# Layer 0's residual held in units of 1/r while down products are added, GpSimd converting it both ways; layer 0's wide product groups ordered in runs of three

## The chip, the cores and the metric

One Trainium2 chip, of which the program uses one core. The metric is device time in microseconds (us) of one execution, lower is better. Beside the timed runs there is one profiled execution, and all durations below are from it.

## The reference, cut to what matters

A two-layer decoder trunk over 512 tokens, model width 1024, float32. Each layer has a mixer and then a gated convolutional FFN of width 2816; each adds its output to the residual `h`. The FFN is the part that the change touches:

```python
hn = rms_norm(h, norm_ffn[layer])          # h times r per token, times a gain per feature
g  = causal_dwconv3(hn @ w_gate, conv_w) + conv_b
h  = h + (silu(g) * (hn @ w_up)) @ w_down
```

The factor r of the norm is one number per token. It has to be inside the silu, so the gate takes it before the convolution. The up branch is linear in it, so r may be applied to the up product, to the gate's result, or to the whole output of the down product.

## The kernel before, in words

**Layout.** Features lie on the 128 partitions, tokens along the free axis. `h` is eight tiles of 128x512 (`h[0]` to `h[7]`), and the factor is a 128x512 tile `self.r` (`rstd_f` in the trace) with the same row on every partition, written by ScalarE (L222). Matrix products are float32 made of three products of a high and a low part: `hi` is a rounded copy by ScalarE, `lo` the rest, made either on VectorE (a subtraction, L152 or L857) or by a copy of minus the source on ScalarE and an adding DMA that GpSimd issues (`summed`, L141 to L145, and L887 to L889).

**The FFN of a layer.** `Ffn.steps` goes over the 22 column tiles of the FFN by two: f = 0, 2, 4, ... 20. f = 0 is computed directly (`direct`). From f = 2 on, gate and up are made by seven products of half size each (a block scheme), fourteen products a step, in `products` (L903 to L984), after `prepare` (L861) has loaded the weights, added and subtracted blocks on VectorE and split them. Between these steps stand groups of the down projection (`half_down`): two tiles after f = 2 and f = 4, four tiles after each later step, each for one half of the model width. Their results are added to `h` by VectorE (L314, `done` of `project`). The last four tiles of layer 0 go down in `d_last`, after f = 20, and there the next norm is begun.

**Wide products.** In most steps the two products with a high part as the stationary operand are made in one pass of 512 columns (high and low parts of the moving operand beside each other), and the product with the low part in one of 256 columns. `in_both` says where: in layer 0 wholly from f = 8, in layer 1 wholly from f = 6. Where a step is wholly wide, layer 1 orders the passes in runs of three (three of 256 columns, then three of 512, L949); layer 0 alternates pairs (L954).

**Who applies r.** In layer 1 the factor is given to the sum in the down step (`add`, L1371). In layer 0 VectorE multiplies: in `direct` each of the two gate results (L791); in `products` the second gate result (L971) and the first two up blocks (L973), beside the row that goes into the convolution, which both layers multiply (L968).

**What sets the order.** The program text gives a priority; a planner builds each engine's queue from it, taking at each free moment the first ready instruction by its own cost model. `behind(a, b)` asks that a stand after b in the queue, without a wait. On the chip every engine then takes its queue in order: GpSimd's holds the adding DMAs, so whatever stands in front of one delays it. `last_added[0]` is the last adding DMA of `summed`. Buffers: seven PSUM banks turn for all products, four `raw`, six `whi`, six `wlo`.

Of the kernel before, what the change touches and what calls it, by code (L numbers as in the profile page):

```python
# [8 lines left out]
F32 = mybir.dt.float32  # L9
# [3 lines left out]
ALU = mybir.AluOpType  # L13
PSUM = bass.MemoryType.PSUM

P = 128
D = 1024
S = 512
NK = D // P
NT = S // P  # L20
FF = 2816
NF = FF // P
# [9 lines left out]
def tile_trunk(ctx: ExitStack, tc: tile.TileContext, x, norm_mix, norm_ffn, final_norm,  # L32
# [3 lines left out]
    nc = tc.nc  # L36
# [9 lines left out]
    def mm_bank(name):  # L46
        return ps_mm.tile([P, 512], F32, tag="mm", name=name)
# [33 lines left out]
    def behind(ins, first):  # L81

        if first is not None:
            tc.add_manual_dep(ins.ins, first.ins.name, mybir.DependencyInfo(
                mybir.DependencyClass.NoSync, mybir.DependencyReason.DATA), reason="order")
# [49 lines left out]
    last_added = [None]  # L135
# [49 lines left out]
    h = [cp.tile([P, S], F32, tag=f"h{k}", name=f"h{k}") for k in range(NK)]  # L185
# [3 lines left out]
    def hg_k(k):  # L189
        return hg[k][0], hg[k][1]  # L190
# [525 lines left out]
    class Ffn:  # L716
# [52 lines left out]
        def direct(self, ch, before):  # L769

            layer = self.layer
            banks = {}
            for i, k in enumerate(PAIRS):
                for j in range(4):
                    before(i, j)
                    hi, lo = ch["gu"[j // 2], i // 4]
                    c = slice((j % 2) * P, (j % 2 + 1) * P)
                    if j not in banks:
                        banks[j] = mm_bank(f"gu{layer}_{j}")
                    mm3(banks[j], (hi[:, i % 4, c], lo[:, i % 4, c]), hg_k(k),  # L780
                        i == 0, i == NK - 1)

            def evacuate():
                r = self.r
                gates = []
                for j in range(2):
                    t = padded_tile()
                    nc.vector.tensor_tensor(t[:, 2:], banks[j], r, ALU.mult)
                    s = self.silu(self.conv(t, j), j)
                    if layer == 0:  # L790
                        nc.vector.tensor_tensor(s, s, r, ALU.mult)  # L791
                    gates.append(s)
                for j, s in enumerate(gates):
                    nc.vector.tensor_tensor(s, banks[2 + j], s, ALU.mult)
                return [(j, s) for j, s in enumerate(gates)]

            return evacuate
# [114 lines left out]
        def products(self, f, stat):  # L912

            layer, ap, n = self.layer, self.ap, f"{self.layer}_{f}"
            banks = {"g": {}, "u": {}}
            kept = ap.tile([P, 3, HALF], F32, tag="kept", bufs=1, name=f"kept{n}")
            pads = [padded_tile() for _ in range(2)]
            lo, hi = slice(2, 2 + HALF), slice(2 + HALF, 2 + S)
            dst = {("g", 1): pads[0][:, lo], ("g", 6): pads[0][:, hi], ("g", 7): pads[1][:, hi],
                   ("g", 4): pads[1][:, lo]}  # L920
            dst.update({("u", product): kept[:, i, :] for i, product in enumerate((1, 6, 7))})
            onto = {2: 1, 7: 7, 3: 6}
            s = {}

            def in_both(key, product):
                first = FIRST_WIDE[layer]
                return f >= first[key] or f == first["g"] and product in (2, 5, 3)

            def add(d, bank, halves):
                ins = None  # L930
                for half in halves:
                    ins = nc.vector.tensor_tensor(d, bank[:, half * HALF : (half + 1) * HALF], d,
                                                  ALU.add)
                return ins

            def after(key, product, bank):
                halves = range(1 + in_both(key, product))
                if product in onto:
                    ins = add(dst[key, onto[product]], bank, halves)
                    if product == 7:  # L940
                        self.added[key] = ins
                elif (key, product) != ("u", 4):
                    d = dst[key, 7 if product == 5 else product]
                    nc.scalar.copy(d, bank[:, :HALF])
                    add(d, bank, halves[1:])

            todo = [("g", 1), ("u", 1), ("g", 2), ("g", 5), ("g", 6), ("u", 5), ("u", 6),
                    ("g", 7), ("u", 2), ("u", 7), ("g", 3), ("u", 3), ("g", 4), ("u", 4)]
            if layer and all(in_both(*at) for at in todo):  # L949
                parts_of = [(0, (False,))]  # L950
                for i in range(0, len(todo), 3):
                    parts_of += [(j, (True,)) for j in range(i, min(i + 3, len(todo)))]
                    parts_of += [(j, (False,)) for j in range(i + 1, min(i + 4, len(todo)))]
            else:  # L954
                parts_of = [(i, (i % 2 == 1, i % 2 == 0)) for i in range(len(todo))]
            begun = set()
            for i, lows in parts_of:
                key, product = todo[i]
                bank = self.multiply(banks[key], f"{key}{n}", product, stat[key, product],
                                     in_both(key, product), lows)  # L960
                if len(lows) == 1 and i not in begun:
                    begun.add(i)
                    continue
                after(key, product, bank)
                if (key, product) in (("g", 4), ("g", 3)):
                    j = product == 4
                    row = pads[j][:, 2:]
                    nc.vector.tensor_tensor(row, row, self.r, ALU.mult)  # L968
                    s[j] = self.silu(self.conv(pads[j], f + j), f + j)
                    if j and layer == 0:  # L970
                        nc.vector.tensor_tensor(s[1], s[1], self.r, ALU.mult)  # L971
            if layer == 0:
                nc.vector.tensor_tensor(kept[:, :2, :], kept[:, :2, :],  # L973
                                        self.r.rearrange("p (a b) -> p a b", a=2), ALU.mult)
            s0 = s[0].rearrange("p (a b) -> p a b", a=2)
            nc.vector.tensor_tensor(s0, kept[:, :2, :], s0, ALU.mult)
            nc.vector.tensor_tensor(s[1][:, HALF:], kept[:, 2, :], s[1][:, HALF:], ALU.mult)
            last = bank[:, :HALF]
            if in_both("u", 4):
                last = kept[:, 0, :]  # L980
                nc.scalar.copy(last, bank[:, :HALF])
                add(last, bank, (1,))
            nc.vector.tensor_tensor(s[1][:, :HALF], last, s[1][:, :HALF], ALU.mult)
            return [(f + 1, s[1]), (f, s[0])]  # L984

        def hidden(self, f, before=lambda i, j: None):

            if f == 0:
                def first(i, j):
                    before(i, j)  # L990
                    if (i, j) == (3, 0):
                        nc.vector.tensor_copy(self.cols, self.norm.rstd_cols(inorder))
                    elif (i, j) == (6, 0):
                        self.r = self.norm.rstd_spread(inorder)

                ch = self.pair_weights([("g", 0), ("u", 0), ("g", 1), ("u", 1)])
                rest = self.direct(ch, first)
                for kp in range(NP):
                    self.block_sums(kp)
                self.second = self.prepare(2)  # L1000
                return rest()
            return self.products(f, self.second if f == 2 else self.prepare(f))

        def steps(self, half_down, before=lambda i, j: None):
# [11 lines left out]
        def split_acts(self, rows):  # L1016
            for ft, row in rows:
                self.act(ft, row)

    def ffn0(norm):  # L1020
        nonlocal prm1
        with tc.tile_pool(name="f0", bufs=1) as ap:
            def sums(kp):
                return [ap.tile([P, 2, HALF], F32R, name=f"t{i}_{kp}") for i in (2, 3)]

            ffn = Ffn(0, prm0, norm, ap, sums)
            def half_down(a, b, half):
                project(f"d0_{a}", w_ffn_down[0], ffn.acts, list(range(a, b)), None,
                        halves=(half,), tail=0)

            ffn.split_acts(ffn.steps(half_down))
            prm1 = params1(lambda ins: behind(ins, last_matmul[0]))
            nxt = Norm("m1", lambda k: prm1("mix", k))
            project("d0_last", w_ffn_down[0], ffn.acts, list(range(NF - 4, NF)), nxt)
            return nxt
# [588 lines left out]
```

## Time and profile before

| what | value |
|---|---|
| timed runs, median of 3 | 967.45 us (966.96 to 967.5) |
| the profiled execution's own time | 967.03 us |
| its span, first to last instruction | 965.2 us |
| TensorE (PE) busy | 956.3 us, 99% of the span |
| VectorE (DVE) busy | 847.2 us, 88% |
| ScalarE (ACT) busy | 619.9 us, 64% |
| GpSimd (POOL) busy | 162.3 us, 17% |
| granted TensorE clock | 0.997 |

How to read it: a row of the timeline has start, duration, engine, line of the kernel, operation, out<-in, shapes, and in brackets the idle time in front of it and who ended that. Where a row merges several instructions (x3), the duration is that of all. A row of a group has the count, then busy time and the mean in ns of one. A tile's name has no number of its step (`s12g` is that of every f), but PSUM banks have: `g_4b` is a bank of the gate at f = 4.

### The profile page before, as it was taken

Reading aid. Unit: us, or ns where it says so; the run is one execution under the profiler, and the core shown is the slowest. Engines: PE = TensorE matmul, PEld = TensorE weight load, DVE = VectorE, ACT = ScalarE, POOL = GpSimd, SP = SyncE. Lnnn points to the kernel's source line nnn. Section 1 sums busy time; section 2 is a strip of 40 time slices with the busy share of each in tenths; the row PEclk is TensorE's granted clock in tenths of the full one; section 3 lists DMA queues with packets and bytes.
Section 4 is the critical chain, followed back from the end, with each engine's and each line's share of the span. In section 5 each row is a group of like instructions: output and inputs, shape, how many; then the busy total and the mean of one; then the engine's idle time right before and its main releaser. Section 6 shows DMA issues by size and latency. Waiting matters only on the chain.

```text
span 965.2 us, 14237 instructions
## 1 busy us (share of the span) xinstructions
PE 956.3 (99%) x5155; PEld 826.9 (86%) x5155; DVE 847.2 (88%) x1435; ACT 619.9 (64%) x943; POOL 162.3 (17%) x184
## 2 busy tenths in 40 slices
PE   9999999999999999999999999999999999999996
PEld 7888898998888888888888888989888888888885
DVE  6887998989898998998878689889998989989897
ACT  5524667766575665765487847787665566646776
POOL 3141333111011010110311002321110011100123
PEclk9999999999999999999999999999999999999998
DMA  7442355787677677774452323567776777667865
GB/s 253 153 134 87 66 152 117 178 191 181 166 178 169 158 178 191 168 180 133 131 153 88 109 88 88 142 137 181 183 185 175 179 175 174 173 164 181 203 148 147
DMA packets 95537, 150.45 MB, mean 156 GB/s; under 512 B 5252, under 2 KB 61036, under 8 KB 95468
## 3 DMA queue, kind: packets, MB, share of 16 engines
q1 hardware_dynamic: 78140, 98.69, 32.9%
q0 software_dynamic: 15696, 49.03, 27.8%
q10 hardware_dynamic: 1632, 1.84, 0.6%
q8 instruction: 40, 0.66, 0.3%
q14 instruction: 29, 0.24, 0.1%
HBM read 98.42 MB, written 2.10 MB: 104 GB/s over the span
## 4 chain that ended last, share of the span: by engine, by line
PE 98%; DVE 1%; DMA 1%; issue 0%; ACT 0%; ACTq 0%
PE dn L156 3%; PE d L156 3%; PE d L157 3%; PE dn L157 3%; PE dn L158 3%; PE d L158 3%; PE vu_a L1166 2%; PE gu L156 2%; PE gu L158 2%; PE gu L157 2%; PE u_2a L705 1%; PE u_4a L705 1%; PE g_2a L705 1%; PE u_20a L695 1%; PE u_18a L695 1%; PE u_8a L695 1%
## 5 line engine op out<-in xcount | busy, mean ns | idle before, releaser
L143 POOL DMA_DIRECT2D wlo_g<-raw_g x20 | 17.2, 859 | 318.8 <-ACT wlo_g L141 95.0
L741 DVE SCALAR_TENSOR_TENSOR c<-rows,prm,c 128x512 f32<-128x512 f32 x88 | 65.2, 750 | 1.4 <-ACT c L739 1.2
L156 PE MATMUL d<-a_hi,whi_d 128*128 128x512 f32 x144 | 56.2, 390 | 0.0
L156 PE MATMUL dn<-whi_dn,a_hi 128*128 128x512 f32 x144 | 56.1, 390 | 0.0
L157 PE MATMUL d<-a_lo,whi_d 128*128 128x512 f32 x144 | 56.1, 390 | 0.0
L157 PE MATMUL dn<-wlo_dn,a_hi 128*128 128x512 f32 x144 | 56.1, 390 | 0.0
L158 PE MATMUL d<-a_hi,wlo_d 128*128 128x512 f32 x144 | 56.1, 389 | 0.0
L158 PE MATMUL dn<-whi_dn,a_lo 128*128 128x512 f32 x144 | 56.1, 389 | 0.0
L856 ACT ACTIVATE whi_a<-raw_g 128x512 fp32r<-128x512 f32 x20 | 12.6, 632 | 67.3 <-PE g_18e L695 9.4
L739 ACT ACTIVATE c<-rows,prm 128x512 f32<-128x512 f32 x44 | 31.3, 714 | 10.6 <-DVE rows L968 10.6
L1371 DVE SCALAR_TENSOR_TENSOR y<-dn,small,y 128x512 f32<-128x512 f32 x40 | 28.0, 749 | 6.6 <-PE dn L158 6.6
L749 ACT ACTIVATE s<-c,prm 128x512 f32<-128x512 f32 x44 | 31.4, 716 | 3.1 <-DVE c L741 3.0
L265 ACT ACTIVATE a_hi<-s 128x512 fp32r<-128x512 f32 x40 | 24.8, 626 | 12.0 <-PE d L158 9.4
L201 ACT ACTIVATE hg<-h,prm 128x512 fp32r<-128x512 f32 x24 | 17.3, 719 | 23.5 <-DVE h L314 17.0
L158 PEld LDWEIGHTS d<-a_hi,wlo_d 128*128 128x128 f32 x144 | 27.1, 188 | 5.6
L158 PEld LDWEIGHTS dn<-whi_dn,a_lo 128*128 128x128 f32 x144 | 27.0, 188 | 5.6
L156 PEld LDWEIGHTS d<-a_hi,whi_d 128*128 128x128 f32 x144 | 27.1, 188 | 5.6
L157 PEld LDWEIGHTS dn<-wlo_dn,a_hi 128*128 128x128 f32 x144 | 27.1, 188 | 5.6
L156 PEld LDWEIGHTS dn<-whi_dn,a_hi 128*128 128x128 f32 x144 | 27.1, 188 | 5.6
L157 PEld LDWEIGHTS d<-a_lo,whi_d 128*128 128x128 f32 x144 | 27.1, 188 | 5.5
L141 ACT ACTIVATE wlo_g<-raw_g 128x1024 fp32r<-128x1024 f32 x20 | 21.0, 1049 | 16.4 <-PE g_2e L705 7.7
L888 POOL DMA_DIRECT2D wlo_s34g<-s34g x18 | 15.5, 860 | 90.9 <-ACT wlo_s34g L887 64.6
(1280 smaller groups left out, 3387.7 us busy)
## 6 DMA issues: line engine op xcount, KB each, us to landing
raw_g<-in_w_ffn_gate_dram SPq DMA_DIRECT2D x40, 512.0 KB, 3.8
raw_u<-in_w_ffn_up_dram SPq DMA_DIRECT2D x40, 512.0 KB, 3.7
raw_dn<-in_w_ffn_down_dram SPq DMA_DIRECT2D x22, 512.0 KB, 3.6
wlo_g<-raw_g POOLq DMA_DIRECT2D x20, 512.0 KB, 5.2
wlo_u<-raw_u POOLq DMA_DIRECT2D x20, 512.0 KB, 6.1
raw_d<-in_w_ffn_down_dram SPq DMA_DIRECT2D x18, 512.0 KB, 4.1
wlo_s12g<-s12g POOLq DMA_DIRECT2D x18, 512.0 KB, 6.6
wlo_s34g<-s34g POOLq DMA_DIRECT2D x18, 512.0 KB, 5.6
```

What stands on the lines that cost most here:

```text
L141: first = nc.scalar.activation(lo, raw, AF.Copy, scale=-1.0)
L156: nc.tensor.matmul(ps, lhs[0], rhs[0], start=start, stop=False, skip_group_check=skip)
L157: nc.tensor.matmul(ps, lhs[0], rhs[1], start=False, stop=False, skip_group_check=skip)
L158: nc.tensor.matmul(ps, lhs[1], rhs[0], start=False, stop=stop, skip_group_check=skip)
L265: nc.scalar.activation(hi, src, AF.Copy, scale=scale)
L695: last_matmul[0] = nc.tensor.matmul(ps if low else banks[at], left(kp)[low], right(kp)[0] if low else both(kp), start=first, stop=kp == NP ...
L705: nc.tensor.matmul(ps, l, r, start=first, stop=end, skip_group_check=True)
L739: nc.scalar.activation(c, t[:, 0:S], AF.Copy, scale=prm("cf", ft))
L741: self.last_conv = nc.vector.scalar_tensor_tensor(c, t[:, i : S + i], prm("cf", i * NF + ft), c, op0=ALU.mult, op1=ALU.add)
L749: self.last_silu = nc.scalar.activation(s, c, AF.Silu, bias=self.prm("bf", ft))
L1166: nc.tensor.matmul(banks[at], lhs[l], rhs[r], start=first, stop=end, skip_group_check=True)
L1371: return nc.vector.scalar_tensor_tensor(dst, ps, ffn.cols[:, t : t + 1], dst, op0=ALU.mult, op1=ALU.add)
```

## The change

Before the first down group, layer 0's `h` is divided by r: VectorE makes `inverse` = 1/r (128x512) and GpSimd multiplies the eight `h` tiles by it, placed behind `prepare(2)`'s last adding DMA. While `h` is held so, down products are added without r, so the multiplications L791, L971 and L973 fall away for f = 0 to 16. For f = 18 and 20 they stay, since these tiles go down in `d_last`, by which time `h` has been multiplied by r again: four tiles on GpSimd after each half of the group that ends at tile 17. And layer 0's wholly wide steps (f = 8 to 20) take the order in runs of three.

```diff
                     s = self.silu(self.conv(t, j), j)
-                    if layer == 0:
-                        nc.vector.tensor_tensor(s, s, r, ALU.mult)
                     gates.append(s)
...
+            scale_up = layer == 0 and f >= NF - 4
...
-            if layer and all(in_both(*at) for at in todo):
+            if all(in_both(*at) for at in todo):
...
-                    if j and layer == 0:
+                    if j and scale_up:
                         nc.vector.tensor_tensor(s[1], s[1], self.r, ALU.mult)
-            if layer == 0:
+            if scale_up:
                 nc.vector.tensor_tensor(kept[:, :2, :], kept[:, :2, :],
                                         self.r.rearrange("p (a b) -> p a b", a=2), ALU.mult)
...
-                return rest()
+                rows = rest()
+                if self.layer == 0:
+                    self.unscale()
+                return rows
...
+        def unscale(self):
+            inverse = self.ap.tile([P, S], F32, name="inverse")
+            nc.vector.reciprocal(inverse, self.r)
+            for k in range(NK):
+                behind(nc.gpsimd.tensor_tensor(h[k], h[k], inverse, ALU.mult), last_added[0])
+
+        def rescale(self, half):
+            for k in range(4 * half, 4 * half + 4):
+                nc.gpsimd.tensor_tensor(h[k], h[k], self.r, ALU.mult)
...
                 project(f"d0_{a}", w_ffn_down[0], ffn.acts, list(range(a, b)), None,
                         halves=(half,), tail=0)
+                if b == NF - 4:
+                    ffn.rescale(half)
```

## The prediction

> **What bounds the kernel now.** I read the page first, its busy times and its chain.
>
> ```profile
> span 965.2 us, 14237 instructions
> ...
> PE 956.3 (99%) x5155; PEld 826.9 (86%) x5155; DVE 847.2 (88%) x1435; ACT 619.9 (64%) x943; POOL 162.3 (17%) x184
> ...
> PE 98%; DVE 1%; DMA 1%; issue 0%; ACT 0%; ACTq 0%
> ```
>
> TensorE stands on 98% of the chain that ended last. VectorE's 88% costs nothing until TensorE waits for it. So the change can gain only where it makes TensorE's own work shorter or takes away one of its few waits, and it can lose wherever it makes an operand late. What the new order is worth can be read in this profile, because layer 1 has it and layer 0 has not. The chain of waits in order of time shows the same place of successive steps:
>
> ```profile
> 279.25 1.41 PE u_10a L695 x8
> ...
> 310.19 1.41 PE u_12a L695 x8
> ...
> 340.63 1.41 PE u_14a L695 x8
> ...
> 804.63 1.41 PE u_12a L695 x8
> 835.03 1.41 PE u_14a L695 x8
> ```
>
> A wide step of layer 0 in pairs takes 340.63 - 310.19 = 30.44 us, one of layer 1 in runs of three 835.03 - 804.63 = 30.40 us. One step of layer 0 is longer, f = 10: 310.19 - 279.25 = 30.94 us, so 0.50 more. The timelines of TensorE and VectorE show why:
>
> ```profile
> 293.90 0.69 DVE L877 TENSOR_TENSOR s12g<-raw_g,raw_g 128x512 f32<-128x512 f32 x1 [2.88 <-DMA raw_g<-in_w_ffn_gate_dram]
> ...
> 296.24 0.74 PE L695 MATMUL u_10a<-t,wlo_u 128*128 128x256 f32 x4 [0.23 <-DVE kept L932]
> ```
>
> VectorE stood 2.88 us for a late load, the emptying of a PSUM bank stood behind it in the queue, and TensorE waited for the bank.
>
> Then I looked at how much room VectorE has, in windows one step long: f = 2 with its down group, f = 4 with its own, and f = 20 (columns: length, PE, PEld, DVE, ACT, POOL busy with counts, clock, DMA).
>
> ```profile
> 165.50:191.13 25.63, 25.63 (x195) 24.67 (x194) 25.43 (x42) 20.34 (x32) 3.44 (x4) 1.00 0.69 166
> 191.13:216.59 25.46, 25.46 (x193) 24.51 (x192) 22.58 (x38) 18.12 (x28) 3.44 (x4) 1.00 0.82 197
> ...
> 430.41:460.85 30.44, 30.44 (x162) 26.18 (x160) 26.93 (x47) 16.04 (x24) 0.02 (x1) 1.00 0.54 148
> ```
>
> In the window of f = 2, VectorE is busy 25.43 of 25.63 us. That is the very place where the division by r is put.
>
> **What goes.**
>
> ```profile
> L971 DVE TENSOR_TENSOR s<-s,rstd_f 128x512 f32<-128x512 f32 x10 | 6.9, 692 | 0.0
> L973 DVE TENSOR_TENSOR kept<-kept,rstd_f 128x512 f32<-128x512 f32 x10 | 6.9, 690 | 0.0
> ...
> 173.01 0.42 DVE L932 TENSOR_TENSOR rows<-g_2b,rows 128x256 f32<-128x256 f32 x1
> 173.42 1.31 DVE L791 TENSOR_TENSOR s<-s,rstd_f 128x512 f32<-128x512 f32 x2
> ```
>
> Eight of ten in each group (f = 2 to 16) and both at L791: 16 x 0.69 + 1.31 = 12.4 us of VectorE. It is off the chain, since VectorE was early everywhere but at f = 10; I price it at nothing for the time, but it counts as room below. The order in runs is 7 steps (f = 8 to 20) x 0.04 = 0.3 us of TensorE. The 0.50 us at f = 10 begins with a load, which the change doesn't touch; I leave it in the sum and keep -0.5 for the range.
>
> **What comes: 1/r.** No 128x512 reciprocal is in the trace. The nearest rows:
>
> ```profile
> L1499 DVE RECIPROCAL ssf<-ssf 128x1 f32<-128x1 f32 x4 | 0.7, 163 | 0.8 <-ACT ssf L1495 0.8
> L246 DVE RECIPROCAL rc_m0c<-sd_m0c x1: 178/178/178, 31.2 to 31.2; 128x4 f32<-128x4 f32 x1
> ```
>
> Three elements more cost 15 ns, 5 ns each: my estimate for 512 is 0.16 + 512 x 0.005 = 2.7 us. From below it is bounded by a multiplication of that shape, 0.69. [...] Place: its text stands behind `prepare(2)` and the gates of f = 0, ahead of the products of f = 2. In the row at 173.01 VectorE takes the first instruction of lower priority than that (a bank of f = 2) while it waits for the gates. There the reciprocal goes in, and ends at 173.0 + 2.7 = 175.7.
>
> **What comes: eight multiplications on GpSimd.**
>
> ```profile
> L533 POOL TENSOR_TENSOR ac<-ac,rstd_m 128x512 f32<-128x512 f32 x4 | 9.8, 2459 | 21.2 <-issue 20.5 <-DVE pl L513 0.7
> ...
> 479.42 1.29 POOL L212 TENSOR_TENSOR ssq_m<-ssq_m,sq_m 128x512 f32<-128x512 f32 x1 [2.87 <-ACT sq_m L211]
> ...
> 52.17 7.51 POOL L533 TENSOR_TENSOR ac<-ac,rstd_m 128x512 f32<-128x512 f32 x3 [0.70 <-DVE pl L513]
> ```
>
> The same operation and shape takes 1.29 us beside a quiet VectorE, and 7.51 / 3 = 2.50 us in a row beside a busy one. In that stretch VectorE suffers too:
>
> ```profile
> 49.01 0.68 DVE L509 SCALAR_TENSOR_TENSOR pl<-zs,z 128x512 f32<-128x512 f32 x1
> ...
> 52.70 1.22 DVE L152 TENSOR_TENSOR wlo_av<-raw_av,whi_av 128x1024 fp32r<-128x1024 f32 x1
> ...
> 54.44 0.69 DVE L505 TENSOR_TENSOR zs<-zs 128x521 f32<-128x521 f32 x1
> ...
> 55.66 1.19 DVE L505 TENSOR_TENSOR zs<-zs 128x513 f32<-128x513 f32 x1
> ...
> 57.36 1.18 DVE L509 SCALAR_TENSOR_TENSOR pl<-zs,z 128x512 f32<-128x512 f32 x1
> 58.46 2.30 DVE L152 TENSOR_TENSOR wlo_ab<-raw_ab,whi_ab 128x1024 fp32r<-128x1024 f32 x1
> ```
>
> Three instructions with two SBUF inputs are lengthened by 0.50, 0.50 and 1.08, so 0.69 us of VectorE for each of GpSimd's three; those that read PSUM are not. [...]
>
> For the eight I take the middle of 1.29 and 2.50, 1.9 us, since the window of f = 2 holds both kinds of VectorE work: GpSimd is done at 175.7 + 8 x 1.9 = 190.9. Ends: 186.0 and 195.7.
>
> **Who waits behind them.** GpSimd's queue is in order, and the multiplications stand ahead of f = 4's adding DMAs (earlier in the text, and ready earlier). GpSimd's timeline, and the views of the two tiles:
>
> ```profile
> 182.74 0.86 POOL L143 DMA_DIRECT2D wlo_g<-raw_g  x1 [14.97 <-ACT wlo_g L141]
> 184.18 0.86 POOL L888 DMA_DIRECT2D wlo_s12g<-s12g  x1 [0.58 <-ACT wlo_s12g L887]
> ...
> L705 PEld LDWEIGHTS g_4b<-hg,wlo_g x4: 192/192/192, 194.0 to 195.0; 128*128 128x128 f32 x4
> ...
> DMA to landing us min/median/max: 6.0/6.0/6.0
> ...
> L705 PEld LDWEIGHTS g_4e<-t,wlo_s12g x4: 192/192/193, 195.4 to 196.5; 128*128 128x128 f32 x4
> ...
> DMA to landing us min/median/max: 7.1/7.1/7.1
> ```
>
> Before, `wlo_g` lands at 188.7 for a use at 194.0, `wlo_s12g` at 191.3 for 195.4. After, issued at 190.9 and 191.8, they land at 196.9 and 198.9: 2.9 and 3.5 us late. TensorE stalls once, **+3.5 us**. By the ends of the multiplication: 186.0 gives nothing, 195.7 gives 195.7 + 0.86 + 7.1 - 195.4 = 8.3. With a reciprocal of 0.69 instead, 1.5.
>
> VectorE's own account points the same way. To f = 4's `wlo_s12u` it gets +2.7 + 8 x 0.69 - 1.31 - 0.69 = +6.2 us.
>
> ```profile
> L857 DVE TENSOR_TENSOR wlo_s12u<-s12u,whi_s12u x1: 1218/1218/1218, 193.7 to 193.7; 128x1024 fp32r<-128x1024 f32 x1
> L705 PEld LDWEIGHTS u_4e<-t,wlo_s12u x4: 192/193/193, 198.3 to 199.4; 128*128 128x128 f32 x4
> ```
>
> It ended at 194.9 for a use at 198.3, room for 3.4, so 2.8 late. That is the same stall of TensorE and isn't added. After it both engines have caught up: the later windows give back 1.38 us a step.
>
> **The way back.**
>
> ```profile
> 461.42 1.28 DVE L314 TENSOR_TENSOR h<-d,h 128x512 f32<-128x512 f32 x2
> 462.62 1.29 DVE L267 TENSOR_TENSOR a_lo<-s,a_hi 128x512 fp32r<-128x512 f32 x2
> ```
>
> The first four multiplications by r fall into f = 20, where no adding DMA is behind them (POOL busy 0.02) and VectorE has 30.44 - 26.93 = 3.5 us for 4 x 0.69 = 2.8: nothing, and the runs of three find their banks emptied as layer 1's do; if that cover is gone, up to 2.8. The last four start as the sums at 461.42 end, beside the two splits at 462.62 that `d_last` is about to read: between nothing and 2 x 0.69 = 1.4; I take 0.5.
>
> **The sum.** +3.5 + 0.5 - 0.3 = +3.7 us on the profiled execution's 967.03: 970.7. The three timed runs have a median of 967.45, 0.42 above it; I add half of that: **970.9 us**.
>
> **The rivals.** (1) The multiplications are hidden: GpSimd is free by 187.4 (195.4 - 7.1 - 0.86), so at under 1.46 us each, or with the reciprocal placed a few us earlier. For it speak the rows of 1.29, and that the planner could find a hole for the reciprocal once the factor is there; against it, that VectorE has 0.2 us idle in that window. Then only -0.3 is left, -0.8 with the wait at f = 10 gone, +0.2 to +1 with a little lost in the way back: 966.4 to 968.5, at its likeliest 967.0. Not slower; it decides at 187.4. [...] (3) Faster by more than 0.2%: 1.9 us would be needed, and the visible gains are 0.3 and 0.5; only a kinder order of the whole plan could bring it. (4) The planner doesn't keep the runs of three: 0.3 less gained, inside the others.
>
> **How the numbers follow.** Forecast 0.45 (969.2 to 973.5), rival 2 0.11 (973.5 to 977), rival 1 0.41 (966.2 to 969.2), rival 3 0.03. A measurement of this kernel can tell about 0.2% from no change, 1.9 us. So faster 0.03, same 0.41, slower 0.56. The range over both signs: 966.4 to 974.5, leaving out rival 3, the lower tail of rival 1 and most of rival 2. The forecast's own range is 969.2 to 973.5.
>
> **What would show it.** GpSimd: eight multiplications in a row from about 176, each clearly over 1.29, and `wlo_g` of f = 4 issued after 188 instead of at 182.74. TensorE: one stall of 2 to 5 us between 182 and 200, then steps of 30.40. VectorE: one reciprocal of 2 to 4 us near 173. It is wrong if the reciprocal stands before 170 or the multiplications end by 187, if the adding DMAs stand ahead of them in the queue, or if TensorE gets over 1 us back anywhere else.

## The result, and the profile after

| | before | after |
|---|---|---|
| timed runs, median of 4 | 967.28 us (966.96 to 967.5) | 979.3 us (978.76 to 979.47) |
| the profiled execution | 967.03 us | 979.25 us |
| its span | 965.2 us | 977.3 us |

After is slower, 1.0124 times before (95% interval 1.0111 to 1.0136). The direction is the forecast's; the size is not: +12.0 us against +3.5, outside the range. First the page of after, busy times and chain:

```profile
span 977.3 us, 14250 instructions
...
PE 959.2 (98%) x5155; PEld 828.8 (85%) x5155; DVE 852.4 (87%) x1418; ACT 618.5 (63%) x943; POOL 188.5 (19%) x200
...
PE 91%; DVE 5%; ACT 2%; issue 1%; DMA 1%; SPq 0%; ACTq 0%; DVEq 0%
```

VectorE has 17 instructions fewer and is busy 5 us longer. The chain, all but TensorE's own before, now runs over VectorE and ScalarE for 7% of the span. Where, the windows of after say: f = 2 with its down group, the next step, f = 20, and 4.3 us inside f = 2 (columns as before):

```profile
166.30:202.49 36.19, 28.26 (x194) 26.69 (x194) 34.65 (x42) 20.93 (x31) 17.52 (x12) 0.91 0.47 114
202.49:227.95 25.46, 25.46 (x193) 24.50 (x193) 21.21 (x36) 17.64 (x27) 3.42 (x4) 1.00 0.83 203
440.90:471.34 30.44, 30.44 (x162) 26.20 (x161) 28.51 (x47) 15.81 (x25) 5.89 (x5) 1.00 0.48 133
184.80:189.10 4.30, 4.29 (x20) 4.30 (x21) 3.71 (x6) 4.29 (x11) 0.00 (x0) 0.50 0.41 120
```

f = 2 takes 36.19 us instead of 25.63: **10.56 of the 12.1 us by which the span grew are in one step**. f = 4 and f = 20 are as they were. The wide steps, by one place of successive steps in the chain (the later place, which the prediction took in layer 1):

```profile
307.20 1.41 PE u_10a L695 x8
...
337.59 1.41 PE u_12a L695 x8
```

Each step is 30.39 us now, 0.05 less than in pairs. The longer step at f = 10 is gone too; from the first product of f = 4 to that of `d_last` TensorE gains 0.89 us. `d_last` then takes 1.45 more. The remaining 0.8 lies ahead of the first product, before anything that was changed. So 0.8 + 10.56 - 0.89 + 1.45 + 0.15 at the end = 12.07, the whole difference of the spans.

TensorE's waits in after:

```profile
PE u_2b L705 <- DVE rows L931: 6.0, 1, 6.0
PE g_2a L705 <- ACT rows L943: 1.2, 1, 1.2
PE d_last L157 <- DVE a_lo L267: 0.9, 1, 0.9
...
PE g_2e L705 <- DVE rows L788: 0.7, 1, 0.7
```

Three waits, 7.9 us, are in f = 2, and each is for a PSUM bank that VectorE or ScalarE had not yet emptied. None is for a DMA. ScalarE was late because of VectorE: its copy out of `g_2a`'s bank stands in its queue behind one that waited 4.6 us for VectorE's sums:

```profile
170.68 1.06 ACT L854 ACTIVATE whi_s12u<-s12u 128x1024 fp32r<-128x1024 f32 x1 [4.61 <-DVE s12u L877]
```

VectorE's timeline across that place:

```profile
164.53 3.35 DVE L1024 RECIPROCAL inverse<-rstd_f 128x512 f32<-128x512 f32 x1
167.79 1.16 DVE L855 TENSOR_TENSOR wlo_s34g<-s34g,whi_s34g 128x1024 fp32r<-128x1024 f32 x1
168.87 1.78 DVE L877 TENSOR_TENSOR s12u<-s12u,raw_u 128x512 f32<-128x512 f32 x1
170.57 1.28 DVE L788 TENSOR_TENSOR rows<-gu,rstd_f 128x512 f32<-128x512 f32 x2
171.77 2.35 DVE L855 TENSOR_TENSOR wlo_s12u<-s12u,whi_s12u 128x1024 fp32r<-128x1024 f32 x1
174.16 1.66 DVE L896 TENSOR_TENSOR s12u<-raw_u 128x512 f32<-128x512 f32 x1
175.74 1.78 DVE L898 TENSOR_TENSOR s12u<-raw_u,s12u 128x512 f32<-128x512 f32 x1
177.44 3.45 DVE L741 SCALAR_TENSOR_TENSOR c<-rows,prm,c 128x512 f32<-128x512 f32 x2
180.81 2.28 DVE L855 TENSOR_TENSOR wlo_s34u<-s12u,whi_s34u 128x1024 fp32r<-128x1024 f32 x1
...
184.34 0.41 DVE L931 TENSOR_TENSOR rows<-g_2b,rows 128x256 f32<-128x256 f32 x1
```

and GpSimd's, with the last four multiplications of the way back:

```profile
167.96 14.05 POOL L1026 TENSOR_TENSOR h<-h,inverse 128x512 f32<-128x512 f32 x8 [0.73 <-DVE inverse L1024]
194.09 0.88 POOL L143 DMA_DIRECT2D wlo_g<-raw_g  x1 [12.08 <-ACT wlo_g L141]
...
470.87 5.93 POOL L1030 TENSOR_TENSOR h<-h,rstd_f 128x512 f32<-128x512 f32 x4 [24.55 <-DVE h L314]
```

Read them together. The reciprocal stands at 164.53, not at 173.0: among the sums and splits of f = 2, right after r was there. It takes 3.35 us, 3.26 to the next start. Then GpSimd multiplies from 167.96 to 182.01, 1.76 us each. Every instruction of VectorE with two SBUF inputs that begins inside that time is longer than its like outside (0.69 us, and 1.22 for the splits of 1024 columns): by 1.09, 1.13, 0.97, 1.09, twice 1.04, and 1.06, together 7.4 us. The pair at 170.57, which reads PSUM, is not (1.28 here and in before). So `g_2b`'s bank is emptied at 184.34 instead of 173.01: 11.33 later, of which 0.8 is the later start of the whole run, and 3.26 + 7.4 = 10.7 accounts for the rest. Seven banks turn for all products, so TensorE's `u_2b` waits for that one:

```profile
184.81 0.79 PE L705 MATMUL u_2b<-hg,whi_u 128*128 128x256 f32 x2 [6.02 <-DVE rows L931]
```

Its first pair of matmuls takes 0.79 us, the later ones 0.63, where such a pair took 0.40 before the stall: the window 184.80:189.10 has a granted clock of 0.50. In it three matmuls start every 0.64 us, before the stall every 0.36. By that some 1.9 of the 4.3 us are lost, which is an estimate. 7.9 + 1.9 is 9.8 of the 10.56; the rest is busy time of TensorE outside that window, and was not taken apart.

### The profile page after: what moved, and what is told of

It reads as the page before. It is cut to its first block, busy times and chain, and to the rows that moved or that the text cites. A ratio compares the mean times of both kernels' runs of the same rounds, so it can differ in the third digit from the quotient of the medians.

```text
span 977.3 us, 14250 instructions
## 1 busy us (share of the span) xinstructions
PE 959.2 (98%) x5155; PEld 828.8 (85%) x5155; DVE 852.4 (87%) x1418; ACT 618.5 (63%) x943; POOL 188.5 (19%) x200
## 4 chain that ended last, share of the span: by engine, by line
PE 91%; DVE 5%; ACT 2%; issue 1%; DMA 1%; SPq 0%; ACTq 0%; DVEq 0%
PE d L156 3%; PE dn L156 3%; PE d L157 3%; PE dn L157 3%; PE d L158 3%; PE dn L158 3%; PE vu_a L1180 2%; PE gu L156 2%; PE gu L158 1%; PE gu L157 1%; PE u_4a L705 1%; PE u_16a L695 1%; PE g_16a L695 1%; PE u_14a L695 1%; PE g_14a L695 1%; PE u_10a L695 1%
## 5 line engine op out<-in xcount | busy, mean ns | idle before, releaser
L145 ACT ACTIVATE whi_u<-raw_u 128x1024 fp32r<-128x1024 f32 x20 | 21.1, 1054 | 19.9 <-PE d L157 10.6
L314 DVE TENSOR_TENSOR h<-d,h 128x512 f32<-128x512 f32 x40 | 26.3, 687 | 6.7 <-PE d L158 6.7
```

The costliest lines, as they stand in the source:

```text
L145: behind(nc.scalar.activation(hi, raw, AF.Copy), first)
L314: nc.vector.tensor_tensor(h[k], ps, h[k], ALU.add)
```

## The experiments

Three causes were open after the result. **The place:** the conversion stands on the emptying of f = 2's banks, and elsewhere it would be cheap. **The time:** the reciprocal and about 1 us of VectorE for each multiplication of GpSimd, which any step would pay. **The queue:** the adding DMAs behind GpSimd's multiplications, which the forecast had. The letters of the theories change their meaning from one group of expectations to the next; in that of the spread kernel, A is the place and B the time. A result without a number of runs is one run. The first runs take the conversion apart.

**No conversion** (both calls left out, so that tiles 0 to 17 go into `h` without the factor):

```diff
-                if self.layer == 0:
-                    self.unscale()
...
-                if b == NF - 4:
-                    ffn.rescale(half)
```

> Left out: the reciprocal and all sixteen multiplications of h, so down products are added without r to an undivided h. What is left is the gain alone: fewer VectorE multiplications and the runs of three. Every theory that puts the loss into the conversion expects f = 2 to take the 25.6 us of before (first product of f = 2 to first product of f = 4), steps of 30.40 us from f = 8 on, no wait at f = 10, and 966.2 to 966.9 us, 0.4 to 1.0 under the kernel before. If the order in runs or the missing multiplications themselves disturbed the plan, it would stay over 968.

Measured: 967.61 us (967.05 to 968.68, 11 runs), 1.0004 times before (0.9995 to 1.0013). In the profile f = 2 takes 25.62 us, and there is no wait at f = 10. So the whole loss hangs on the conversion. But 967.61 is above the 966.2 to 966.9 that was expected, and what is left does not gain either: 0.90 us are won from f = 4 to `d_last`, and 0.55 of them go in `d_last`, which comes earlier and waits 0.3 for ScalarE's rounded copy, and 0.32 between the value product and the output product of layer 1.

**The reciprocal alone** (no multiplications, in or back) and **the multiplications alone** (by r, there being no reciprocal):

```diff
-            for k in range(NK):
-                behind(nc.gpsimd.tensor_tensor(h[k], h[k], inverse, ALU.mult), last_added[0])
```
```diff
-            inverse = self.ap.tile([P, S], F32, name="inverse")
-            nc.vector.reciprocal(inverse, self.r)
...
-                behind(nc.gpsimd.tensor_tensor(h[k], h[k], inverse, ALU.mult), last_added[0])
+                behind(nc.gpsimd.tensor_tensor(h[k], h[k], self.r, ALU.mult), last_added[0])
```

> Left out: all sixteen multiplications of h; the reciprocal stays at its place in VectorE's queue. Theory A (reciprocal 3.35 us, and then eight multiplications that exclude VectorE's two-input instructions, about 7.3 us together; TensorE has slack for 3 to 4 us of VectorE, not for 10.7): f = 2 takes 25.6 to 26.5 us, 966.3 to 967.5 in all. Theory B (the reciprocal's place in front of the sums of f = 2 does it, the multiplications run beside the work): f = 2 takes over 33 us, 974 or more.

> Left out: the reciprocal; GpSimd multiplies h by r instead of 1/r, eight times at the start and eight at the end. Theory A: VectorE's two-input instructions beside the eight multiplications are lengthened by about 7 us together, the bank of g_2b is emptied 3 to 4 us too late, f = 2 takes 28 to 31 us (25.6 before), and d_last loses 1.4 as in the changed kernel: 970 to 973. Theory B: f = 2 takes 25.6 to 26.5, 967 to 968.5.

Measured, one run of each: 969.03 us with f = 2 at 27.73 us, and 976.32 us with f = 2 at 34.02. Both are above what was expected of them. The one wait of the second in f = 2, and one row of VectorE there, where three such instructions take 2.07 otherwise (ScalarE's copy was late again because ScalarE had itself waited, 3.8 and 1.8 us, for this line of VectorE):

```profile
PE g_2a L705 <- ACT rows L943: 6.7, 1, 6.7
```

```profile
171.46 5.18 DVE L741 SCALAR_TENSOR_TENSOR c<-rows,prm,c 128x512 f32<-128x512 f32 x3
```

What follows: the two parts add up, 2.1 + 8.4 = 10.5 against 10.56. VectorE's additional time in the three kernels (the reciprocal, the multiplications, both) is 3.3, 7.3 and 10.7 us, TensorE's waiting in f = 2 is 1.3, 6.7 and 7.9. So the room at this place was 2.0, 0.6 and 2.8 us and not 3.4: the reciprocal alone already stops TensorE. The rest of each loss, up to 2.1, 8.4 and 10.6, is longer busy time of TensorE. In after some 1.9 of it fall at the clock of 0.50; over the whole execution the granted clock was 0.995 in after and with the multiplications alone, and 0.998 with the reciprocal alone.

**The reciprocal where the forecast had it**, behind the last gate product:

```diff
-                    nc.vector.tensor_tensor(s, banks[2 + j], s, ALU.mult)
+                    self.last_gate = nc.vector.tensor_tensor(s, banks[2 + j], s, ALU.mult)
...
-            nc.vector.reciprocal(inverse, self.r)
+            behind(nc.vector.reciprocal(inverse, self.r), self.last_gate)
```

> The whole change, but the reciprocal stands behind the last gate product of f = 0 in VectorE's queue, about where the forecast had placed it. Theory C (the forecast: with the reciprocal there the multiplications end after 188, the adding DMAs of f = 4 are issued late, and TensorE stalls at g_4b or g_4e): those DMAs are issued 8 us or more after the ones of the kernel before relative to f = 4's start, f = 2 with its down group takes 25.6 to 27, and f = 4 with its own 29 to 31 instead of 25.6; 971 to 974. Theory A alone: f = 2's last evacuations and f = 4's sums are late instead, f = 2 takes 28 to 32, and f = 4 stays within 1 us of before; 970 to 974. Theory B: under 969.

Measured: 976.16 us. The reciprocal starts at 175.11, GpSimd is done at 192.58, and f = 4's adding DMA stands behind it, as forecast:

```profile
178.54 14.04 POOL L1026 TENSOR_TENSOR h<-h,inverse 128x512 f32<-128x512 f32 x8 [10.31 <-DVE inverse L1024]
192.52 0.86 POOL L143 DMA_DIRECT2D wlo_g<-raw_g  x1
```

```profile
PE g_4b L705 <- DVE h L314: 3.8, 1, 3.8
PE g_4e L705 <- DMA wlo_s12g<-s12g: 0.7, 1, 0.7
```

```profile
200.46:207.08 6.62, 5.92 (x28) 5.63 (x27) 5.41 (x10) 5.14 (x9) 0.85 (x1) 0.50 1.07 248
```

f = 2 is 0.6 us longer and f = 4 7.6, which is the pattern of theory C, with more than its 29 to 31 us for f = 4. So with the forecast's own place the loss is still 8.2 us, not 3.5. TensorE waits 3.8 us for a bank that VectorE's sums onto `h` set free, then 0.7 for the landing of `wlo_s12g`, and the 6.6 us that hold this second wait have a clock of 0.50. That costs it some 3 us, an estimate: it is what the two waits leave of the 7.6. This run does not part VectorE from the queue. The DMA behind the one above, and its landing:

```profile
193.10 1.18 POOL L886 DMA_DIRECT2D wlo_s12g<-s12g  x1
```

```profile
DMA to landing us min/median/max: 8.6/8.6/8.6
```

`wlo_g`, ready since 182.9 and held by the queue alone, landed 5.5 us after its issue, 2.9 late, just as forecast. `wlo_s12g` landed at 201.7. Before, TensorE first read this tile 4.6 us after the first product of f = 4, which would be 196.6 here, so the landing was some 5 us late and would have held TensorE about as long without the sums. But VectorE had finished `s12g` only at 191.4 and ScalarE its copy at 192.57, just when GpSimd came free, so without the queue this second DMA would hardly have been earlier. Of the 7.6 that f = 4 loses, 4.5 are waits, and some 3, by the estimate above, are the clock's.

**No way back** (the second conversion left out):

```diff
-                if b == NF - 4:
-                    ffn.rescale(half)
```

> Left out: the second half of the conversion, the eight multiplications by r that bring h back, so d_last is added to an h in the wrong units. If the four of them beside the last two splits cost TensorE its 1.4 us in d_last, this run has d_last at most 0.5 us longer than the kernel before and is 0.9 to 1.2 us under the changed kernel: 977.9 to 978.5. If d_last is longer only because the plan differs, it stays at 1.4 and 979.3.

Measured: 978.01 us; f = 2 is as in after, `d_last` is 0.26 longer than before instead of 1.45. The way back costs 1.2 us. Its mechanism stands in VectorE's timeline of after, ahead of the wait of 0.9 us:

```profile
472.50 3.16 DVE L267 TENSOR_TENSOR a_lo<-s,a_hi 128x512 fp32r<-128x512 f32 x2
```

Two splits take 3.16 us beside the multiplications that began at 470.87; before they took 1.29.

**GpSimd only writes** (24 fills of a spare tile in place of the multiplications; no reciprocal and no way back):

```diff
-            inverse = self.ap.tile([P, S], F32, name="inverse")
-            nc.vector.reciprocal(inverse, self.r)
-            for k in range(NK):
-                behind(nc.gpsimd.tensor_tensor(h[k], h[k], inverse, ALU.mult), last_added[0])
+            spare = self.ap.tile([P, S], F32, name="spare")
+            for k in range(3 * NK):
+                behind(nc.gpsimd.memset(spare, 0.0), last_added[0])
```

> Left out: the reciprocal and all sixteen multiplications; in the place of the first eight GpSimd writes zeros to a spare tile 24 times, so it is busy at the same place (some 13 us by the rows of its small memsets) but reads nothing of SBUF. Theory A1 (the exclusion is between VectorE's second SBUF input and GpSimd's reading): no instruction of VectorE is lengthened, f = 2 takes 25.6 us and the time is 966.4 to 967.8. Theory A2 (any GpSimd work on SBUF holds VectorE up, or its queue does it): VectorE's instructions are lengthened as beside the multiplications, and f = 2 takes over 30 us, 973 or more.

Measured: 967.0 us, f = 2 25.62. GpSimd's row and VectorE's beside it:

```profile
167.53 14.31 POOL L1025 MEMSET spare<- 128x512 f32 x24
```

```profile
168.09 0.69 DVE L896 TENSOR_TENSOR s12u<-raw_u 128x512 f32<-128x512 f32 x1
...
169.30 2.07 DVE L741 SCALAR_TENSOR_TENSOR c<-rows,prm,c 128x512 f32<-128x512 f32 x3
```

GpSimd is as busy and as long as with the multiplications (14.31 us against 14.05), at the same place. From 164 to 180 no row of VectorE is over 0.02 us longer than in before but one: a pair of splits at 174.91 takes 1.48 us instead of 1.29, and it takes 1.48 also with the multiplications alone, where it begins after the last of them. So the loss does not come with GpSimd's work as such: VectorE lost 7.4 us beside eight instructions that read SBUF and write it, and at most 0.2 beside 24 that only write it. That is theory A1's outcome, and the loss is put down to the reading. Whether the two engines exclude each other, as the expectation has it, no run shows; measured are the longer times.

**All sixteen multiplications on VectorE**, which then has no neighbour:

```diff
-                behind(nc.gpsimd.tensor_tensor(h[k], h[k], inverse, ALU.mult), last_added[0])
+                nc.vector.tensor_tensor(h[k], h[k], inverse, ALU.mult)
...
-                nc.gpsimd.tensor_tensor(h[k], h[k], self.r, ALU.mult)
+                nc.vector.tensor_tensor(h[k], h[k], self.r, ALU.mult)
```

> The whole change with VectorE itself making all sixteen multiplications instead of GpSimd. Eight of 0.60 us each are 4.8 us for VectorE at f = 2, while beside GpSimd's eight its own work grew by 7.3. Theory A: f = 2 and f = 4 together lose 3 to 7 us instead of 10.6, and it is under the changed kernel: 970 to 975. If only the room in VectorE's queue counted and GpSimd's multiplications were a relief, it would be as slow or slower: 979 or more.

Measured: 980.91 us, so no better than after; the 970 to 975 of theory A are missed, and the other branch came. The eight on the way in take 0.68 each, 0.60 from one start to the next, so 4.8 us of VectorE's queue, with no other instruction lengthened; f = 2 is 2.4 us longer and f = 4 8.1, 10.5 in sum, and some 3 more are lost later in layer 1. TensorE's longest wait, for a copy that needs VectorE's sums:

```profile
PE g_4a L705 <- ACT whi_s12g L887: 3.1, 1, 3.1
```

This speaks for VectorE's time as the cause, whichever engine multiplies. But the loss does not follow that time closely: it is 3.3 + 4.8 = 8.1 us by the one engine and 3.3 + 7.4 = 10.7 by the other, and TensorE loses the same. The planner put the work behind the multiplications in another order here (the waits stand in f = 4), and what that is worth was not taken apart.

**Another place, and spread** tests the place against the time directly. Tiles 0 and 1 keep the factor on VectorE, and the rest is as its expectation says:

```diff
-            scale_up = layer == 0 and f >= NF - 4
+            scale_up = layer == 0 and f >= NF - 8
...
+                if self.layer == 0 and f in (6, 8, 18, 20):
+                    self.convert(int(f in (8, 20)), f < 10)
...
+        def convert(self, half, down):
+            if down and half == 0:
+                self.inverse = self.ap.tile([P, S], F32, name="inverse")
+                for c in range(0, S, P):
+                    behind(nc.vector.reciprocal(self.inverse[:, c : c + P],
+                                                self.r[:, c : c + P]), self.added["u"])
+            by = self.inverse if down else self.r
+            for i, k in enumerate(range(4 * half, 4 * half + 4)):
+                behind(nc.gpsimd.tensor_tensor(h[k], h[k], by, ALU.mult), added_all[i - 4])
```

> The same conversion at another place and spread out: tiles 0 and 1 keep their factor on VectorE as before, h is divided only between the first quarter of down products and the next one, the reciprocal goes in four pieces of 128 columns behind the last added half of f=6's direct products, the eight multiplications by the reciprocal one behind each of eight adding DMAs of f=8 and f=10, the eight by r one behind each adding DMA about f=18 and f=20; the factor is multiplied on VectorE again from f=14 on. The whole computation is kept. Theory A (the 10.6 us of the change come from the place: eight multiplications in a row and a 3.35 us reciprocal while g_2a to u_2e are evacuated, with under 1 us of slack): one multiplication at a time lengthens one or two instructions of VectorE by about 1 us, f=2 takes 25.6 us, the steps f=6 to f=10 no more than 0.7 us longer each, 967.2 to 970. Theory B (VectorE's lost time, about 3.4 us for the reciprocal and 8 times 1 us each way, is paid wherever it falls): 972 to 979, with the loss in f=6 to f=10 and f=18 to f=20.

Measured: 983.8 us (983.3 to 984.37, 5 runs), 1.0169 times before (1.0155 to 1.0183), above the ranges of both theories. f = 2 is free of it, 25.62 us. But f = 8, f = 18 and f = 20 are these:

```profile
247.82:287.85 40.03, 34.41 (x161) 28.70 (x160) 37.45 (x60) 26.18 (x37) 11.84 (x12) 0.91 0.83 199
409.43:444.40 34.97, 32.49 (x162) 27.45 (x160) 32.88 (x54) 20.56 (x30) 11.28 (x10) 0.95 0.61 150
444.40:477.50 33.10, 31.32 (x162) 26.11 (x161) 31.23 (x51) 16.42 (x26) 2.75 (x3) 1.00 0.58 156
```

The windows begin with the step's first product. In before the step f = 8 was this:

```profile
247.27:277.70 30.43, 30.43 (x161) 26.23 (x160) 27.66 (x51) 18.18 (x28) 2.36 (x3) 1.00 0.63 156
```

So the three are 9.6, 4.5 and 2.7 us longer than 30.4, and VectorE is again what TensorE mostly waits for:

```profile
PE g_8b L697 <- DVE s34g L902: 2.3, 1, 2.3
...
PE u_18e L697 <- DVE wlo_s12u L859: 1.3, 1, 1.3
PE g_18a L697 <- DVE rows L935: 1.2, 1, 1.2
```

GpSimd's first row of the conversion, and VectorE's rows around it:

```profile
240.70 6.86 POOL L1034 TENSOR_TENSOR h<-h,inverse 128x512 f32<-128x512 f32 x4 [21.92 <-DVE inverse L1030]
```

```profile
239.67 0.94 DVE L1030 RECIPROCAL inverse<-rstd_f 128x128 f32<-128x128 f32 x1
240.55 0.75 DVE L743 SCALAR_TENSOR_TENSOR c<-rows,prm,c 128x512 f32<-128x512 f32 x1
...
242.93 1.77 DVE L743 SCALAR_TENSOR_TENSOR c<-rows,prm,c 128x512 f32<-128x512 f32 x1
```

The instruction of L743 takes 0.75 us where it began ahead of the first multiplication, and 1.77 beside the next. **The place alone as the cause falls, the time stands:** f = 8, 80 us behind f = 2 and with VectorE idle for 2.8 of its 30.4 us before, pays the way in with 9.6 us, 5.6 of them as waits and 4.0 as longer busy time of TensorE, with a clock of 0.91 over the step. The multiplications were less spread than meant, since four of the eight ran in a row, 6.86 us.

**The order alone.** The runs of three in the kernel before, nothing else:

```diff
-            if layer and all(in_both(*at) for at in todo):
+            if all(in_both(*at) for at in todo):
```

> Nothing of the conversion: the kernel before with the runs of three in layer 0 alone, so VectorE keeps all its multiplications by r. If layer 0's VectorE is fast enough for the runs (28.5 of 30.4 us a step, as layer 1's), steps of 30.40 and 966.5 to 967.2. If the conversion was needed to make the room, TensorE waits in each of the seven steps for banks, half a microsecond or more, and it is 970 or more.

Measured: 969.34 us (967.26 to 971.61, 7 runs), 1.0026 times before (1.0015 to 1.0037): between the two branches, a little slower, and scattered. The profiled run was the lowest, with steps of 30.39 to 30.51 us and no wait. The same kernel once more, for a run above the lowest:

> The kernel before with the runs of three in layer 0 and nothing else, once more, for a profile of a run above the lowest. If the scatter between 967.3 and 971.6 us comes from this order of the products, a stall of some tenths to 4 us stands in one of the steps f=4 to f=18 at a wide product that waits for a low half or a bank; if it comes from outside, every step is 30.35 to 30.40 us and the difference lies before the layer or behind it. Expected time 967.3 to 969.5 us.

Measured: 970.45 us, 3.2 above the profiled run of the first. TensorE's waits in it, and the landing of f = 20's `wlo_u`, here and then in the first:

```profile
PE u_20b L695 <- DMA wlo_u<-raw_u: 1.2, 1, 1.2
PE g_14a L695 <- DVE rows L932: 0.3, 1, 0.3
PE g_18a L695 <- DVE rows L932: 0.3, 1, 0.3
```

```profile
DMA to landing us min/median/max: 11.4/11.4/11.4
```

```profile
DMA to landing us min/median/max: 9.5/9.5/9.5
```

The stalls stand in the wide steps of layer 0, where the order was changed, and not before the layer. In runs of three `u_20b` is taken 10.2 us after the step's first product, in pairs 12.1. In before the same DMA landed after 6.2 us. By these numbers the pairs' order would have covered the slower landing (12.1 us against some 11.5 from the step's first product), and this one does not; that is an estimate. From the first product of f = 14 to `d_last` this run loses 2.8 us on the other, 0.4 in f = 14, 0.9 in f = 18 and 1.4 in f = 20. In f = 14 and f = 18 the waits are for banks that VectorE empties. So the order in runs wins 0.05 us a step and takes cover from banks and low halves that come at changing times. One such run was seen; that all of the scatter is this is likely, not shown.

Beside it stands the run with no conversion. It has this order as well, but not the multiplications on VectorE that fall away with the change (L791, and L971 and L973 up to f = 16), and it took 967.61, 1.0004 times before against 1.0026 here. So with the new order the multiplications that fall away are worth some 1.7 us. One trace of it shows a way: f = 20's `wlo_u` was issued 1.9 us ahead of the step's first product there, and 0.05 and 0.13 us behind it in the two runs here.

## Why the prediction was wrong, step by step

- **What bounds the kernel** held: TensorE, and in the changed kernel its waits were for banks that were late by VectorE, or by ScalarE behind VectorE.
- **What goes** held in size: seven times 0.05 and the 0.5 at f = 10 that was kept for the range, 0.9 together. That they shorten the end did not hold: without the conversion 0.9 is given back in `d_last` and layer 1. That the two gains together came near the -0.3 of the sum is luck: by the timed runs the order alone costs 2.2 us, and taking the multiplications off VectorE, which was priced at nothing, gives 1.7 of them back.
- **The reciprocal's size:** 2.7 forecast, 3.35 measured, 0.65 us more.
- **The reciprocal's place, the first step that failed:** "In the row at 173.01 ... There the reciprocal goes in". It went in at 164.53, as soon as r was there, which is one of the signs of being wrong that the prediction names. That moved the multiplications from f = 4's DMAs onto f = 2's banks, so the stall came at `u_2b` at 178.8 and not at `g_4b`. By the run with the place put back, it is 2.4 of the 10.6 us.
- **GpSimd's multiplication:** 1.9 forecast, 1.76 measured.
- **VectorE's loss for each:** 0.69 taken from three rows, 0.93 measured over eight in after (7.4 us); about 1.06 there for each instruction that meets one.
- **Who waits behind them, the second step that failed:** "It ended at 194.9 for a use at 198.3, room for 3.4, so 2.8 late. That is the same stall of TensorE and isn't added." The account of VectorE was made at one tile of f = 4, with room for 3.4, and its loss then dropped as the same stall as the DMAs'. The runs showed VectorE behind all of the waiting in f = 2 of after, 7.9 us with none for a DMA, and behind most of it in f = 8 spread out; with the place put back, VectorE and the DMAs are about equally late. In f = 2 the room was 0.6 to 2.8 us and not 3.4, so that a reciprocal alone costs 2.1. The window's 25.43 of 25.63 us was quoted and not used as the room.
- **Left out of the sum, the third step that failed:** the clock after a stall, put at nothing without a reason. A stall of 6.0 us was followed by 4.3 us at a clock of 0.50, some 1.9 us on top. With the place put back it is some 3 us, the larger part of what 8.2 has over 3.5; the waits there, 4.9 us in all, are 1.4 more than forecast.
- **The way back:** 0.5 forecast, 1.2 measured, inside its bounds of 0 and 1.4. The first four were hidden, as forecast: f = 20 takes 30.44 us.
- **The rivals:** the second one's range, 973.5 to 977, comes nearest to the changed kernel, and stays 2.3 us below it. No run shows a term that leads to this range. What the runs showed in its place is 0.93 us of VectorE for a multiplication, room of 0.6 to 2.8 us, and a loss of clock. VectorE did not stand idle while TensorE stalled (178.79 to 184.81): none of its rows between 164.53 and 184.34 shows a wait.

## What to carry to other kernels

Charge an engine's added time at the first operand that its queue makes late, not at the place where the last one of the new work is wanted, and take as room the gap of that operand, not the idle share of a window. Work that was put on GpSimd was paid on VectorE here: beside eight multiplications that read SBUF, VectorE's instructions with two SBUF inputs took 7.4 us longer, more than the 4.8 that the same eight took of its queue when it made them itself. And work that is taken off an engine that was early bought nothing against the kernel before (967.61 without the conversion, 967.22 before), though it made up for an order that left VectorE's operands less cover. So a change that trades twelve such microseconds for ten in a tight place loses the ten.

## What the runs showed of the hardware that was not expected

- A 128x512 reciprocal took 3.35 us on VectorE, in four pieces of 128 columns 0.94 us each; on one column it took 0.16 in the row that the prediction shows.
- A clock of 0.50 came after a shorter stall than the 6.0 us of after, 3.8 us with the reciprocal's place put back, and in one place a clock of 0.60 after two short ones. In the spread kernel two waits of 1.2 and 1.3 us left TensorE busy 0.98 of 3.46 us, and the next 4.2 us had a clock of 0.60:

```profile
414.90:418.36 3.46, 0.98 (x7) 0.57 (x5) 2.67 (x5) 2.37 (x4) 0.00 (x0) 1.00 0.41 77
418.36:422.58 4.22, 4.22 (x13) 3.40 (x14) 4.04 (x8) 2.56 (x5) 0.00 (x0) 0.60 0.48 145
```

  In after, two of 0.7 and 1.2 us with 1.7 us of matmuls between them had no such stretch behind them: the clock stayed at 1.00 up to the stall at 178.8.
- Open: f = 18 and f = 20 of the spread kernel lose 7.2 us to a way back that costs 1.2 in the change. Some of it may be the order in runs, which lost 0.9 and 1.4 there by itself in one run; the rest was not taken apart.
